# mLSTM branch: row sums from ones stored beside the values, and row maxima broadcast by DMA through DRAM

## The chip, the cores and the metric

The kernel runs on one core of a Trainium2 chip. A core has a matrix engine (PE, whose weight loads are shown apart as PEld), a vector engine (DVE), a scalar engine (ACT), GpSimd (POOL), and a queue that only issues DMAs (SP). Matmuls write into PSUM accumulators; DVE and ACT read these and write SBUF; POOL works on SBUF and issues DMAs of its own. The metric is the device time of one execution in microseconds, as the median of several runs. Lower is better.

## The reference, cut to what matters

Two layers, each over 256 tokens of width 2048. A layer projects the normed input into four branches (S5, mLSTM, differential attention, memory cross-attention), gates each, projects it back and merges the four. Everything is in 32-bit floats.

The change touches the mLSTM branch. It has 4 heads of width 256. For head h, with the summed log forget gates `acum`, the input gates `ic` and the running row maximum `m_row`, the reference computes

```
dmat = where(causal, acum_q - acum_k + ic_k, -inf)
s    = (q @ k^T) * exp(dmat - m_row)
num  = s @ v                    den = sum over k of s
h    = num / max(|den|, exp(-m_row))
```

It does so in two chunks of 128 tokens with a carried state. The kernel computes both chunks at once, as three 128 x 128 blocks of the lower triangle: (chunk 0, chunk 0), (chunk 1 rows, chunk 0 keys) and (chunk 1, chunk 1).

## The kernel before, in words

**The main stream.** All weights (944 pieces, called units here, of 128 x 1024 numbers) are loaded in order by SP (`do_load`, L292), split by ACT into a rounded high part `wh` (L303) and by DVE into the rest `wl` (`tt`, L206), and multiplied in three matmuls per product (`mm3`, L356 to L358: high by high, high by low, low by high). `tok_group` uses 12 matmuls of 512 columns per unit, `chan_group` 24 of 256 columns. While PE works on unit i, the split of unit i + 3 (`LA` = 3) is being issued. These high and low parts are of a type that PE takes in one pass.

**The branches run in between.** Each branch is a Python generator. After every unit, `used()` calls `bg_step()`, which advances each live generator by one `yield`: one step per unit. What a step emits goes to each engine's queue behind everything emitted earlier, and each engine works through its queue in that order. `ticks(n, period, stages)` starts head i at step `i * period` and runs stage `f` of a head at its offset. The S5 branch (`s5_gen`) runs along at the same time, with priority behind the mLSTM.

**The mLSTM.** `ml_rows` (L955) computes, some 70 units ahead, a tile `R` (`mlR`) of 128 partitions x 256 tokens: rows 0 to 3 hold the key terms, rows 32 to 35 the row maxima for the denominator, rows 64 to 67 the negated maxima of the four heads. `ml_gen` (L993) transposes `R` on PE, keeps two small pieces, and then per head:

- `s_mm` (offset 0): one matmul with a column of the identity, broadcast over 128 columns, against `R`. It copies row 64 + h of `R` to all 128 partitions of a PSUM tile `pm` (256 columns). Then four matmuls for the scores `k^T q`, into another PSUM tile.
- `s_arg` (offset 1, DVE): three instructions that read `pm` and write the exponents into `mlE`; `s_exp` (ACT) and `s_mul` (DVE) turn them into `s`.
- `o_mm` (offset 6): for each of the three blocks a matmul of `mlE` with the 256 value columns of this head, and one with two columns of ones (`ones2`, in the constants tile `cst`), whose first column is the denominator.
- `o_den` to `y_l` (offsets 7 to 17): normalisation and transposes; the small root of `o_rs` (L434 to L444, L1069) runs on POOL.

These matmuls take plain 32-bit operands. In the trace every such matmul stands as two records (8 heads in all, so `mlR` has 16 records). All helpers share lines: `mmf` is L361, the transpose `tr` L364, DVE's helpers L206 to L214, ACT's L203.

The heads start 16 steps apart. The values `v` lie in `mlv`, 2 x 1024 numbers per partition, written by ACT from PSUM when the value projection of a group of two heads is done.

**POOL's queue** carries the S5 branch's loads (`ur`, `br`, `ct`, `ub`) and stores (`ydr`) as DMAs, the small roots, and a few memsets. **PSUM** has three rotating buffers (`ps`) for all this work.

Of the kernel before, what the change touches and what calls it, by code (L numbers as in the profile page):

```python
# [8 lines left out]
F32 = mybir.dt.float32  # L9
# [148 lines left out]
def body(tc, x, mem, w_in, w_if, w_kv, w_br, w_glu, w_out, cols, s5_b, s5_c, lqk, g_post, consts, out,  # L158
         depth=L, taps=None):
    nc = tc.nc  # L160
    taps = taps or {}
    from contextlib import ExitStack
    with ExitStack() as ctx:
# [791 lines left out]
        def ml_rows(cl, wif, hb, lb, st):  # L955

            yield
            yield
            ifp = acc()
            for kb in range(16):  # L960
                nc.tensor.matmul(ifp[0:100, 0:256], lhsT=wif[:, kb, 0:100], rhs=hb(kb), start=kb == 0, stop=False,
                                 skip_group_check=True)
                nc.tensor.matmul(ifp[0:36, 0:256], lhsT=wif[:, kb, 0:36], rhs=lb(kb), start=False, stop=kb == 15,
                                 skip_group_check=True)
            yield
            bi, bf = pcol(cl, "b_i", 0, 4), pcol(cl, "b_f", 0, 4)
            w = [t2.tile([4, 2, 256], F32, name=f"mlw{i}", tag="t2") for i in range(2)]
            fr, ab, ee, A = w[0][:, 0], w[0][:, 1], w[1][:, 0], w[1][:, 1]
            S.copy(out=fr, in_=ifp[32:36, 0:256])
            S.copy(out=ab, in_=ifp[0:4, 0:256])  # L970
            R = sp.tile([128, 256], F32, name="mlR", tag="mlR")
            P.memset(R, 0.0)
            yield
            stt(fr, ifp[96:100, 0:256], bf, fr, A_, A_)
            stt(R[0:4], ifp[64:68, 0:256], bi, ab, A_, A_)
            ts(fr, fr, -1.0, M_)
            yield
            stt(ab, fr, -1.0, fr, M_, X_)
            act(ee, ab, AF.Exp, scale=-1.0)
            act(ee, ee, AF.Ln, bias=c_one[0:4])  # L980
            yield
            one = C("ones")[0:4, 0:1].to_broadcast([4, 256])
            stt(ee, fr, 0.0, ee, X_, A_)
            V.tensor_tensor_scan(out=A, data0=one, data1=ee, initial=0.0, op0=M_, op1=S_)
            tt(R[0:4], R[0:4], A, S_)
            yield
            V.tensor_tensor_scan(out=ab, data0=one, data1=R[0:4], initial=0.0, op0=M_, op1=X_)
            tt(R[32:36], A, ab, A_)
            ts(R[64:68], ab, -1.0, M_)
            st["R"] = R  # L990
            yield

        def ml_gen(l, cl, st, q8, k8, v, gate, yh, yl):  # L993
            R = st["R"]
            pc = ps()[:, 0:256]
            for t in range(2):
                tr(pc[:, t * 128:t * 128 + 128], R[:, t * 128:t * 128 + 128])
            pcv = pc.rearrange("p (t r) -> p t r", t=2)
            hg = sp.tile([128, 8], F32, name="mlhg", tag="mlhg")
            ts(hg, cl[:, COLS["ml_g"][0]:COLS["ml_g"][1]], 0.5, M_)  # L1000
            G = sp.tile([128, 2, 4], F32, name="mlG", tag="mlG")
            eam = sp.tile([128, 2, 4], F32, name="mleam", tag="mleam")
            V.tensor_copy(G, pcv[:, :, 0:4])
            act(eam, pcv[:, :, 32:36], AF.Exp, scale=-1.0)
            msk = C("maskml")
            yield
            held = {}

            def s_mm(h):
                pm = ps()[:, 0:256]  # L1010
                mmf(pm, ident[:, 64 + h:65 + h].to_broadcast([128, 128]), R, True, True)
                p = ps()[:, 0:384]
                for d in range(2):
                    mmf(p[:, 0:256], k8[:, 2 * h + d, 0:128], q8[:, 2 * h + d, 0:256], d == 0, d == 1)
                for d in range(2):
                    mmf(p[:, 256:384], k8[:, 2 * h + d, 128:256], q8[:, 2 * h + d, 128:256], False, d == 1)
                held[h] = {"pm": pm, "p": p}

            def s_arg(h):
                e = held[h]  # L1020
                pm = e["pm"]
                E = t2.tile([128, 384], F32, name="mlE", tag="t2")
                stt(E[:, 0:128], pm[:, 0:128], G[:, 0, h:h + 1], msk, A_, ALU.min)
                ts(E[:, 128:256], pm[:, 128:256], G[:, 0, h:h + 1], A_, 0.0, ALU.min)
                stt(E[:, 256:384], pm[:, 128:256], G[:, 1, h:h + 1], msk, A_, ALU.min)
                e["E"] = E

            def s_exp(h):
                act(held[h]["E"], held[h]["E"], AF.Exp)

            def s_mul(h):
                e = held[h]
                stt(e["E"], e["p"], 1.0 / 16, e["E"], M_, M_)

            def o_mm(h):
                E = held[h]["E"]
                vs = slice(h * 256, h * 256 + 256)
                pn = [ps(), ps()]
                mmf(pn[0][:, 0:256], E[:, 0:128], v[:, 0, vs], True, True)
                mmf(pn[0][:, 256:258], E[:, 0:128], ones2, False, True)  # L1040
                mmf(pn[1][:, 0:256], E[:, 128:256], v[:, 0, vs], True, False)
                mmf(pn[1][:, 256:258], E[:, 128:256], ones2, False, False)
                mmf(pn[1][:, 0:256], E[:, 256:384], v[:, 1, vs], False, True)
                mmf(pn[1][:, 256:258], E[:, 256:384], ones2, False, True)
                held[h]["pn"] = pn

            def o_den(h):
                e = held[h]
                rec = sm.tile([128, 2], F32, name="mlrec", tag="sm")
                dn = sm.tile([128, 2], F32, name="mldn", tag="sm")  # L1050
                for q in range(2):
                    V.tensor_copy(dn[:, q:q + 1], e["pn"][q][:, 256:257])
                stt(rec, dn, -1.0, dn, M_, X_)
                tt(rec, rec, eam[:, :, h], X_)
                V.reciprocal(out=rec, in_=rec)
                e["rec"] = rec

            def o_sq(h):
                e = held[h]
                y = t2.tile([128, 2, 256], F32, name="mly", tag="t2")  # L1060
                ss = sm.tile([128, 2], F32, name="mlss", tag="sm")
                for q in range(2):
                    act(y[:, q], e["pn"][q][:, 0:256], AF.Square, scale=e["rec"][:, q:q + 1], accum_out=ss[:, q:q + 1])
                e.update(y=y, ss=ss)

            def o_rs(h):
                e = held[h]
                rsqrt(e["ss"], e["ss"], 1.0 / 256, 2, P)
                P.tensor_tensor(out=e["ss"], in0=e["ss"], in1=e["rec"], op=M_)  # L1069

            def o_y(h):
                e = held[h]
                for q in range(2):
                    stt(e["y"][:, q], e["pn"][q][:, 0:256], e["ss"][:, q:q + 1], gate[:, q, h * 256:h * 256 + 256], M_, M_)

            def y_T(h):
                py = ps().rearrange("p (d t) -> p d t", d=2)
                for d in range(2):
                    for q in range(2):
                        tr(py[:, d, q * 128:q * 128 + 128], held[h]["y"][:, q, d * 128:d * 128 + 128])  # L1080
                held[h]["py"] = py

            def y_h(h):
                for d in range(2):
                    act(yh[:, 2 * h + d], held[h]["py"][:, d], AF.Identity, scale=hg[:, 2 * h + d:2 * h + d + 1])

            def y_l(h):
                for d in range(2):
                    stt(yl[:, 2 * h + d], held[h]["py"][:, d], hg[:, 2 * h + d:2 * h + d + 1], yh[:, 2 * h + d], M_, S_)

            yield from ticks(4, 16, [(0, s_mm), (1, s_arg), (2, s_exp), (4, s_mul), (6, o_mm), (7, o_den), (8, o_sq),
                                     (9, o_rs), (12, o_y), (15, y_T), (16, y_h), (17, y_l)])

        def xa_gen(l, qT, kT, v, z, yh, yl):
# [66 lines left out]
        ydr = dr.tile([8, 128, 256], F32, name="ydr")  # L1161
        kdr = dr.tile([128, 2048], F32, name="kdr")
        vdr = dr.tile([128, 2048], F32, name="vdr")

        def seq(*fns):

# [50 lines left out]
        for l in range(depth):  # L1217
# [93 lines left out]

            mlst = {}
            bg_add(ml_rows(cl, wif, hb, lb, mlst))
            mv = big("mlv").rearrange("p (t d) -> p t d", t=2)
            mg = big("mlg").rearrange("p (t d) -> p t d", t=2)

            def z_gen(o, g):
# [11 lines left out]
            for c0, dst, fn in ((MLV, mv, AF.Copy), (MLO, mg, AF.Tanh), (MLZ, None, None)):  # L1329
                for g in range(2):  # L1330
# [1 line left out]
                    if dst is None:  # L1332
                        bg_add(z_gen(o, g))
                    else:
                        evac(lambda o=o, g=g, dst=dst, fn=fn: [
                            act(dst[:, t, g * 512:g * 512 + 512], o[t], fn, scale=0.5 if fn == AF.Tanh else 1.0)
                            for t in range(2)])
            cq = big("mlq").rearrange("p (b t) -> p b t", b=8)
            ck = big("mlk").rearrange("p (b t) -> p b t", b=8)

# [279 lines left out]
```

## Time and profile before

| | |
|---|---|
| median of 3 runs | 2814.99 us (2811.59 to 2815.05) |
| the profiled execution | 2815.6 us, of which its span is 2813.8 us |
| PE busy | 2796.6 us, 99% |
| DVE busy | 1999.0 us, 71% |
| ACT busy | 1491.1 us, 53% |
| POOL busy | 274.4 us, 10% |
| granted PE clock | 0.998 |
| the mLSTM heads in layer 0, layer 1 | about 590 to 790 us, 1988 to 2190 us |

Busy time on PE counts a matmul from its start to its modelled end, and matmuls overlap; what one costs is read from the distance between starts, or from the chain of work that ended last, which gives each matmul only the time by which it moves the end. Each engine's busy share over the span hides stages: what a change is worth is read in the stretch where it acts. A time in this text is counted from the start of the span.

### The profile page before, as it was taken

The numbers are of one execution on the slowest core, as the hardware profiler recorded it, in microseconds if no ns is written. First come the engines' busy times: TensorE is split into PE (matmuls) and PEld (weight loads), VectorE is DVE, ScalarE is ACT, GpSimd is POOL, SyncE is SP. The second block draws the span as 40 slices with busy tenths as digits, with TensorE's granted clock in tenths as the row PEclk, the third lists the DMA queues.
The fourth block names the chain that finished last, engine by engine and source line by source line (L and its number), as shares of the span: only waits on it lengthen the run. The fifth ranks groups of instructions, "written<-read, shape, count | busy, mean of one in ns | idle before, by whom it ended". The sixth has DMA issues, their size and how long they took to land.

```text
span 2813.8 us, 41302 instructions
## 1 busy us (share of the span) xinstructions
PE 2796.6 (99%) x15604; PEld 2422.6 (86%) x15604; DVE 1999.0 (71%) x3068; ACT 1491.1 (53%) x2116; POOL 274.4 (10%) x594
## 2 busy tenths in 40 slices
PE   9999999999999999999999999999999999999998
PEld 7988878988998898887889888789889988988887
DVE  6678787787778875555575787877887778665555
ACT  6445665465555544444454556655655555444443
POOL 1010122011110000000010102220112000000000
PEclk9999999999999999999999999999999999999999
DMA  7666556555565556556566665565555655566555
GB/s 253 222 207 200 171 163 196 189 181 189 174 223 178 180 188 209 189 188 225 211 221 212 208 195 175 165 196 184 190 183 175 224 166 189 191 209 203 189 189 183
DMA packets 164840, 547.31 MB, mean 195 GB/s; under 512 B 32192, under 2 KB 32576, under 8 KB 162336
## 3 DMA queue, kind: packets, MB, share of 16 engines
q1 hardware_dynamic: 141408, 512.60, 54.5%
q0 software_dynamic: 23232, 32.08, 4.1%
q8 instruction: 122, 2.00, 0.3%
q14 instruction: 78, 0.64, 0.1%
HBM read 531.80 MB, written 12.58 MB: 193 GB/s over the span
## 4 chain that ended last, share of the span: by engine, by line
PE 96%; DVE 2%; issue 0%; DMA 0%; POOL 0%; ACT 0%; SPq 0%; DVEq 0%; ACTq 0%; POOLq 0%
PE acc L356 30%; PE acc L357 30%; PE acc L358 30%; PE ps L361 3%; PE ps L364 2%; DVE wl L206 1%; PE yps L361 1%; PE ps L753 1%; DMA memt<-in_mem 0%; ACT wh L303 0%; POOL rz L442 0%; DVE s5b L206 0%; DVE s5a L206 0%; DVE o L214 0%; DVE das L214 0%
## 5 line engine op out<-in xcount | busy, mean ns | idle before, releaser
L206 DVE TENSOR_TENSOR wl<-raw,wh 128x1024 fp32r<-128x1024 f32 x942 | 1150.7, 1223 | 755.8 <-ACT wh L303 752.1
L303 ACT CAST wh<-raw 128x1024 fp32r<-128x1024 f32 x942 | 987.9, 1050 | 1212.8 <-PE acc L358 814.3
L356 PE MATMUL acc<-wh,hh 128*128 128x512 f32 x1920 | 759.1, 395 | 0.0
L357 PE MATMUL acc<-wl,hh 128*128 128x512 f32 x1920 | 748.5, 390 | 0.5 <-DVE wl L206 0.5
L358 PE MATMUL acc<-wh,hl 128*128 128x512 f32 x1920 | 748.4, 390 | 0.0
L356 PE MATMUL acc<-hh,wh 128*128 128x256 f32 x1536 | 435.7, 284 | 0.0
L357 PE MATMUL acc<-hl,wh 128*128 128x256 f32 x1536 | 434.6, 283 | 0.0
L358 PE MATMUL acc<-hh,wl 128*128 128x256 f32 x1536 | 434.6, 283 | 0.0
L356 PEld LDWEIGHTS acc<-wh,hh 128*128 128x128 f32 x1920 | 360.8, 188 | 78.5 <-issue 6.5
L358 PEld LDWEIGHTS acc<-wh,hl 128*128 128x128 f32 x1920 | 360.4, 188 | 76.8
L357 PEld LDWEIGHTS acc<-wl,hh 128*128 128x128 f32 x1920 | 361.0, 188 | 71.2 <-DVE wl L206 1.1
L356 PEld LDWEIGHTS acc<-hh,wh 128*128 128x128 f32 x1536 | 294.8, 192 | 1.9 <-issue 1.6
L357 PEld LDWEIGHTS acc<-hl,wh 128*128 128x128 f32 x1536 | 294.8, 192 | 0.2
L358 PEld LDWEIGHTS acc<-hh,wl 128*128 128x128 f32 x1536 | 294.8, 192 | 0.0
L356 PE MATMUL acc<-wh,th 128*128 128x512 f32 x248 | 98.2, 396 | 0.0
L357 PE MATMUL acc<-wl,th 128*128 128x512 f32 x248 | 97.2, 392 | 0.0
L358 PE MATMUL acc<-wh,tl 128*128 128x512 f32 x248 | 97.1, 392 | 0.0
L674 POOL DMA_DIRECT2D ur<-udr x64 | 44.4, 693 | 515.0 <-DVE bs L206 491.2
L203 ACT ACT_TABLE_LOAD x67 | 86.0, 1283 | 6.7 <-DMA cols<-in_cols 3.3
L434 POOL TENSOR_SCALAR rq<-rq 128x2 f32<-128x2 f32 x28 | 7.3, 261 | 789.4 <-DVE rz L430 789.4
L771 DVE TENSOR_TENSOR_SCAN s5b<-s5r,s5a 128x256 f32<-128x256 f32 x128 | 81.1, 674 | 0.1
L356 PE MATMUL acc<-mh,wh 128*128 128x256 f32 x256 | 73.8, 288 | 0.0
(314 smaller groups left out, 3742.6 us busy)
## 6 DMA issues: line engine op xcount, KB each, us to landing
raw<-in_w_in SPq DMA_DIRECT2D x672, 512.0 KB, 3.4
raw<-in_w_br SPq DMA_DIRECT2D x128, 512.0 KB, 3.4
raw<-in_w_kv SPq DMA_DIRECT2D x64, 512.0 KB, 3.4
raw<-in_w_out SPq DMA_DIRECT2D x64, 512.0 KB, 3.3
raw<-in_w_glu SPq DMA_DIRECT2D x16, 512.0 KB, 4.3
ur<-udr POOLq DMA_DIRECT2D x64, 96.0 KB, 5.0
br<-in_s_b POOLq DMA_DIRECT2D x64, 96.0 KB, 5.6
memt<-in_mem SPq DMA_DIRECT2D x16, 256.0 KB, 7.0
```

The lines of the kernel that those rows point to most:

```text
L203: return S.activation(out=out, in_=in_, func=func, **kw)
L206: return V.tensor_tensor(out=out, in0=a, in1=b, op=op)
L303: S.copy(out=h, in_=r)
L356: nc.tensor.matmul(o, lhsT=ah, rhs=bh, start=start, stop=False, skip_group_check=True)
L357: nc.tensor.matmul(o, lhsT=ah, rhs=bl, start=False, stop=False, skip_group_check=True)
L358: nc.tensor.matmul(o, lhsT=al, rhs=bh, start=False, stop=stop, skip_group_check=True)
L361: nc.tensor.matmul(o, lhsT=lhsT, rhs=rhs, start=start, stop=stop, skip_group_check=True)
L364: nc.tensor.transpose(o, i, ident)
L434: E.tensor_scalar(out=m, in0=m, scalar1=-0.5, scalar2=None, op0=M_)
L674: nc.gpsimd.dma_start(out=ur, in_=udr[c // 4, rows].unsqueeze(0).to_broadcast([3, 32, 256]))
L753: nc.tensor.matmul(pb[:, ri], lhsT=e["bs"][:, ri], rhs=e["us"], start=ri == 0, stop=True, skip_group_check=True)
L771: V.tensor_tensor_scan(out=e["tb"][:, ri], data0=rb, data1=e["ta"][:, ri], initial=0.0, op0=M_, op1=A_)
```

## The change

Three things are done differently.

- **Ones beside the values.** `mlv` becomes 128 x 2 x 4 x 258: behind the 256 values of each head stand two columns of ones, written once per layer by a memset on POOL. ACT's writes into `mlv` become two blocks of 256 with a gap. `o_mm` then needs one matmul of 258 columns per block in place of one of 256 and one of 2, so its denominator arrives in column 256 of the same PSUM tile as before.
- **Row maxima by DMA.** At the end of `ml_rows` POOL's queue writes rows 64 to 67 of `R` to a DRAM buffer `rdr` (4 x 256). In `ml_gen` a new stage `r_load(h)` loads row h from there into all 128 partitions of an SBUF tile `mlpm` (128 x 256, one buffer). The matmul that made `pm` in PSUM is gone, and `s_arg` reads `mlpm`. Head 0 is loaded before the heads start, head h + 1 at offset 9 of head h.
- **Two steps later.** Behind the first `r_load` stand two extra `yield`s, so that all stages of all heads come two units later in the stream.

```diff
@@ ml_rows
             st["R"] = R
+            nc.gpsimd.dma_start(out=rdr, in_=R[64:68])
             yield
@@ ml_gen
+            def r_load(h):
+                pm = t1.tile([128, 256], F32, name="mlpm", tag="mlpm", bufs=1)
+                nc.gpsimd.dma_start(out=pm, in_=rdr[h].partition_broadcast(128))
+                held[h] = {"pm": pm}
+
             def s_mm(h):
-                pm = ps()[:, 0:256]
-                mmf(pm, ident[:, 64 + h:65 + h].to_broadcast([128, 128]), R, True, True)
                 p = ps()[:, 0:384]
                 ...
-                held[h] = {"pm": pm, "p": p}
+                held[h]["p"] = p
...
                 pn = [ps(), ps()]
-                mmf(pn[0][:, 0:256], E[:, 0:128], v[:, 0, vs], True, True)
-                mmf(pn[0][:, 256:258], E[:, 0:128], ones2, False, True)
-                mmf(pn[1][:, 0:256], E[:, 128:256], v[:, 0, vs], True, False)
-                mmf(pn[1][:, 256:258], E[:, 128:256], ones2, False, False)
-                mmf(pn[1][:, 0:256], E[:, 256:384], v[:, 1, vs], False, True)
-                mmf(pn[1][:, 256:258], E[:, 256:384], ones2, False, True)
+                mmf(pn[0][:, 0:258], E[:, 0:128], v[:, 0, h], True, True)
+                mmf(pn[1][:, 0:258], E[:, 128:256], v[:, 0, h], True, False)
+                mmf(pn[1][:, 0:258], E[:, 256:384], v[:, 1, h], False, True)
...
+            r_load(0)
+            for _ in range(2):
+                yield
             yield from ticks(4, 16, [(0, s_mm), (1, s_arg), ..., (8, o_sq),
+                                     (9, lambda h: h < 3 and r_load(h + 1)),
                                      (9, o_rs), (12, o_y), (15, y_T), (16, y_h), (17, y_l)])
@@ the layer's body
-            mv = big("mlv").rearrange("p (t d) -> p t d", t=2)
+            mv = b8.tile([128, 2, 4, 258], F32, name="mlv", tag="b8")
+            P.memset(mv[:, :, :, 256:258], 1.0)
...
+                                if dst is mv:
+                                    act(mv[:, t, 2 * g:2 * g + 2, 0:256], blk2(o[t]), AF.Copy)
```

On PE, the value product `o_mm` of head 0 in layer 0 stood in the queue like this before (each row is one matmul or a run of equal ones; `mlE` holds `s`, `cst` the ones):

```order
L358 MATMUL acc<-wh,hl 128x512
L361 MATMUL ps<-mlv,mlE 128x256
L361 MATMUL ps<-cst,mlE 128x2
L361 MATMUL ps<-mlv,mlE 128x256
L361 MATMUL ps<-cst,mlE 128x2
L361 MATMUL ps<-mlv,mlE 128x256
L361 MATMUL ps<-cst,mlE 128x2
L356 MATMUL acc<-wh,ydah 128x512
L357 MATMUL acc<-wl,ydah 128x512
```

and so with the change:

```order
L357 MATMUL acc<-wl,ydah 128x512
L358 MATMUL acc<-wh,ydal 128x512
L361 MATMUL ps<-mlv,mlE 128x258 x3
L356 MATMUL acc<-wh,ydah 128x512
L357 MATMUL acc<-wl,ydah 128x512
```

Six matmuls became three, and they stand two units further on. In `s_mm` of the same head (`mlR` is `R`, `mlq` and `mlk` the queries and keys) PE had before

```order
L358 MATMUL acc<-wh,hl 128x512
L361 MATMUL ps<-mlR,cst 128x256
L361 MATMUL ps<-mlq,mlk 128x256 x2
L361 MATMUL ps<-mlq,mlk 128x128 x2
L356 MATMUL acc<-wh,hh 128x512
```

and has with the change

```order
L358 MATMUL acc<-wh,hl 128x512
L361 MATMUL ps<-mlq,mlk 128x256 x2
L361 MATMUL ps<-mlq,mlk 128x128 x2
L356 MATMUL acc<-wh,hh 128x512
```

so only the matmul that reads `R` is gone. POOL's queue, around the loads for heads 0 and 1 in layer 0, reads with the change as follows (in brackets the engines and DMA queues whose progress a row waits for):

```order
L802 DMA ydr<-ub 128x256 [waits DMASW7_49,DVE_49]
L1012 DMA mlpm<-rdr 128x256 [waits DMASW0_49]
L674 DMA ur<-udr 96x1x256 [waits DMASW3_49,DVE_49,Activation_49]
L675 DMA br<-in_s_b 96x1x256 [waits DMASW4_49,DVE_49,Activation_49]
L666 DMA ct<-in_s_c 128x256 [waits PE_49]
L667 DMA ub<-udr 128x256 [waits DMASW7_49]
L674 DMA ur<-udr 96x1x256 [waits DMASW5_49,DVE_49,Activation_49]
L675 DMA br<-in_s_b 96x1x256 [waits DMASW6_49,DVE_49,Activation_49]
L1012 DMA mlpm<-rdr 128x256 [waits DMASW0_49,DVE_49]
L434 TENSOR_SCALAR rq<-rq 128x2 [waits DVE_49]
```

The two rows of L1012 are new; the second stands ahead of the small root of head 0 and waits for DVE, since `mlpm` has one buffer that `s_arg` of head 0 must have read.

More of the change, by code (lines that the diff above doesn't have):

```diff
@@ L1036, in o_mm @@
                 E = held[h]["E"]
-                vs = slice(h * 256, h * 256 + 256)
                 pn = [ps(), ps()]
-                mmf(pn[0][:, 0:256], E[:, 0:128], v[:, 0, vs], True, True)
-                mmf(pn[0][:, 256:258], E[:, 0:128], ones2, False, True)
-                mmf(pn[1][:, 0:256], E[:, 128:256], v[:, 0, vs], True, False)
-                mmf(pn[1][:, 256:258], E[:, 128:256], ones2, False, False)
-                mmf(pn[1][:, 0:256], E[:, 256:384], v[:, 1, vs], False, True)
-                mmf(pn[1][:, 256:258], E[:, 256:384], ones2, False, True)
+                mmf(pn[0][:, 0:258], E[:, 0:128], v[:, 0, h], True, True)
+                mmf(pn[1][:, 0:258], E[:, 128:256], v[:, 0, h], True, False)
+                mmf(pn[1][:, 0:258], E[:, 256:384], v[:, 1, h], False, True)
                 held[h]["pn"] = pn
@@ L1163, in body @@
         vdr = dr.tile([128, 2048], F32, name="vdr")
+        rdr = dr.tile([4, 256], F32, name="rdr")
         def seq(*fns):
@@ L1334, in body, with ev @@
                     else:
-                        evac(lambda o=o, g=g, dst=dst, fn=fn: [
-                            act(dst[:, t, g * 512:g * 512 + 512], o[t], fn, scale=0.5 if fn == AF.Tanh else 1.0)
-                            for t in range(2)])
+                        def ev(o=o, g=g, dst=dst, fn=fn):
+                            for t in range(2):
+                                if dst is mv:
+                                    act(mv[:, t, 2 * g:2 * g + 2, 0:256], blk2(o[t]), AF.Copy)
+                                else:
+                                    act(dst[:, t, g * 512:g * 512 + 512], o[t], fn, scale=0.5)
+                        evac(ev)
             cq = big("mlq").rearrange("p (b t) -> p b t", b=8)
```

## The prediction

> **What bounds the kernel now.** I read the page first, then PE's own waits, then the two stretches of the first mLSTM (590 to 690 and 690 to 790 us) by engine, and last the chain of waits inside them.
>
> ```profile
> span 2813.8 us, 41302 instructions
> PE 2796.6 (99%) x15604; PEld 2422.6 (86%) x15604; DVE 1999.0 (71%) x3068; ACT 1491.1 (53%) x2116; POOL 274.4 (10%) x594
> PE 96%; DVE 2%; issue 0%; DMA 0%; POOL 0%; ACT 0%; SPq 0%; DVEq 0%; ACTq 0%; POOLq 0%
> ```
>
> PE is the bound: it fills the span, and the chain that ended last runs over it for 96%. All that PE waited for in the whole program is this:
>
> ```profile
> PE ps L364 <- DMA memt<-in_mem: 3.4, 2, 2.1
> PE ps L364 <- DVE ydal L214: 2.0, 2, 1.0
> PE ps L361 <- DVE warm L1201: 1.3, 1, 1.3
> PE acc L357 <- DVE wl L206: 0.8, 3, 0.3
> ```
>
> Columns are total us, times, longest. None of these is in the mLSTM heads. There, by stretch (us, then busy us of PE, PEld, DVE, ACT, POOL, clock, DMA share, GB/s):
>
> ```profile
> 590.00:690.00 100.00, 100.00 (x472) 82.73 (x471) 84.23 (x148) 60.49 (x86) 17.53 (x39) 1.00 0.58 184
> 690.00:790.00 100.00, 100.00 (x669) 91.78 (x668) 77.87 (x132) 54.33 (x79) 16.57 (x39) 1.00 0.56 182
> ```
>
> PE has no gap, and the clock is full. So whatever work leaves PE here shortens the program, as long as DVE, which is 84% busy, still delivers the splits `wl` in time. And nothing but shorter PE work can help here: there is no idle time to recover.
>
> **What the removed matmuls cost.** Their records:
>
> ```profile
> L361 PE MATMUL ps<-mlv,mlE 128*128 128x256 f32 x48 | 15.2, 406 | 0.0
> L361 PE MATMUL ps<-cst,mlE 128*128 128x2 f32 x48 | 6.7, 209 | 0.0
> L361 PE MATMUL ps<-mlR,cst 128*128 128x256 f32 x16 | 4.7, 378 | 0.0
> ```
>
> The counts give 24 value products, 24 products with ones and 8 products with `R`, two records each. Adding the busy times of the last two (6.7 + 4.7 = 11.4 us) would overstate the price, since records overlap. The chain gives each group only the time by which it moves the end (start, us, what, records). For `s_mm` and `o_mm` of head 0, each with the matmuls right behind it:
>
> ```profile
> 593.49 1.74 PE ps L361 x10
> 595.23 0.24 PE acc L356
> 595.46 0.23 PE acc L357
> 611.85 1.86 PE ps L361 x12
> 613.71 0.34 PE acc L356
> 614.04 0.23 PE acc L357
> ```
>
> And as a yardstick, `s_mm` of the memory attention, which is four plain 32-bit matmuls of 256 columns and nothing else:
>
> ```profile
> 835.30 1.73 PE ps L361 x8
> 837.03 0.23 PE acc L356
> ```
>
> One such matmul costs 1.73 / 4 = 0.4325 us, and the matmul behind the group pays nothing extra (0.23).
>
> - `R` matmul: 0.43 us per head. `s_mm` goes from 1.74 to 1.31. The four score matmuls stay.
> - Ones: `o_mm` now takes 1.86, of which three value products are 3 x 0.4325 = 1.30; the three pairs of two-column records make up the other 0.56, 0.19 us a pair for 2 columns. Behind them the first matmul of the main stream takes 0.34 in place of 0.23, 0.11 more; behind a group that ends in a wide matmul (837.03, 595.23) it doesn't. So 0.56 + 0.11 = 0.67 per head.
> - The two columns that each value product gains: 2 / 256 of 0.4325 is 0.003 us, 0.01 per head. No row shows a plain matmul of 258 columns. From below it costs the 0.4325 of 256 columns, from above the 0.43 + 0.19 + 0.04 = 0.66 that the pair costs today (if the extra columns were worked off as a piece of their own). I take 0.436, since cost per column is even between the rows at hand, and keep the other end for a rival.
>
> Sum per head: 0.43 + 0.67 - 0.01 = 1.09 us. Eight heads: **8.7 us** off PE.
>
> [...]
>
> **What is added, and what hides it.** DVE's three instructions of `s_arg` now read SBUF.
>
> ```profile
> L214 DVE SCALAR_TENSOR_TENSOR mlE<-ps,mlG,cst 128x128 f32<-128x128 f32 x16 | 5.5, 341 | 0.0
> L206 DVE TENSOR_TENSOR us<-ur,us x64: 416/417/419, 175.0 to 2432.9; 32x256 fp32r<-32x256 f32 x64
> L206 DVE TENSOR_TENSOR lq<-lq x4: 217/218/225, 272.0 to 1672.0; 128x64 f32<-128x64 f32 x4
> ```
>
> From PSUM one takes 0.34; from SBUF, 64 columns take 0.22 and 256 take 0.42, so 128 lie between: at most 8 x 3 x 0.08 = 1.9 us more on DVE over the program, at most 2.9 less. I take nothing. ACT writes the same 512 numbers per instruction into `mlv`, only with a gap in them; I take nothing there too.
>
> Whether DVE's work is hidden is a matter of the lead with which a split is ready. Counting splits and units from the start (944 of each), the smallest lead in either layer's heads is this one:
>
> ```profile
> 728.83 1.23 DVE L206 TENSOR_TENSOR wl<-raw,wh 128x1024 fp32r<-128x1024 f32 x1 [2.11 <-ACT wh L303]
> 733.66 0.28 PE L357 MATMUL acc<-hl,wh 128*128 128x256 f32 x1
> ```
>
> Ready at 730.06, used at 733.66: 3.6 us. Most others have 5 to 8. PE takes 1.1 us per head less, once in 16 units, and DVE catches up within a head, as it is idle for 16 of 100 us. So the lead covers the faster PE, and the two-step shift of every stage merely moves the same DVE work among other splits.
>
> POOL gets 8 loads, 2 stores and 2 small memsets. The nearest transfers are the S5 loads, and `lq`, which copies one row of 256 numbers to 128 partitions just as the new load does (KB, us from issue to landing; then the least, median and most for `ur`):
>
> ```profile
> ur<-udr POOLq DMA_DIRECT2D x64, 96.0 KB, 5.0
> lq<-in_lqk POOLq DMA_DIRECT2D x2, 128.0 KB, 4.9
> DMA to landing us min/median/max: 3.4/5.0/7.1
> 575.87 0.57 POOL L667 DMA_DIRECT2D ub<-udr  x1
> 622.03 0.22 POOL L434 TENSOR_SCALAR rq<-rq 128x2 f32<-128x2 f32 x1 [45.59 <-DVE rz L430]
> ```
>
> `mlpm` lands some 5 us (3.4 to 7.1) after its issue. For head 0 POOL stood idle from 576 to 622 us, and its load waits only for a store made 200 us earlier; `s_arg` runs after 598. For the others the load is emitted 8 steps ahead of `s_arg`; a step is 12 matmuls of 0.23 us, so 8 are 22 us. Cover is 22 - 0.6 - 5 = 16 us, and if that were used up, the 3.6 us of lead would come next. Behind the load in POOL's queue stands only the root of the head before, needed three steps (8 us) later. So the price is nothing.
>
> The store of `R` and the memset fall into the one stretch where PE is short of splits:
>
> ```profile
> 381.12 0.50 PE L357 MATMUL acc<-wl,hh 128*128 128x512 f32 x1 [0.27 <-DVE wl L206]
> 378.63 0.28 DVE L210 TENSOR_SCALAR mlR<-mlw 4x256 f32<-4x256 f32 x1
> 385.23 0.23 POOL L434 TENSOR_SCALAR rq<-rq 128x2 f32<-128x2 f32 x1 [20.30 <-DVE rz L430]
> ```
>
> The store can go at 379 and takes under 0.8 us of POOL, which sits idle until 385. If it came 0.6 us in the way in both layers, it would cost 1.2 us; I take nothing and keep that.
>
> **Sum.** The profiled execution took 2815.6 us, 1.8 around its span. 2815.6 - 8.7 = 2806.9. It stands 0.6 above the median of the runs, so the median of the changed kernel should be **2806.3 us**, 0.31% less. A difference of 0.2% (5.6 us) is about what a measurement of this kernel can tell from no change.
>
> **The rivals.**
>
> - *The splits run out.* In 590 to 690 us, where heads 0 and 1 run, DVE is 84% busy. If the faster PE ate the lead there, PE would wait for `wl` and the first two heads of each layer would give their gain back: 4 x 1.09 = 4.4 us, time 2810.7. For it: the DVE share, and PE has waited for `wl` at 381 us. Against: leads of 3.6 us and more against 1.1 per head. Chance 0.10.
> - *A 258-column matmul costs as much as the pair.* Then only the `R` matmul pays, 8 x 0.43 = 3.5 us: 2811.5. This is also the case in which the ones were never worth removing. Nothing in the rows shows a step in cost at 256 columns. Chance 0.05.
> - *Two-column records are nearly free*, by their columns, and the 0.56 us belongs to something that stays, such as the change between operand types. Then 3.5 us from `R` and the 0.11 behind each `o_mm`, 0.9: 2810.6. Against: the yardstick group changes types as well and leaves nothing over. [...] Chance 0.05.
> - *The broadcast comes late, and the kernel is slower.* `s_arg` would hold DVE's queue, the split of the next unit stands behind it, and PE starves. It begins when `mlpm` lands more than 22 us after its turn, and costs PE from 22 + 3.6 on; the kernel is slower by over 0.2% when each head loses 1.09 + 0.7, that is at 27.4 us and more. At 30 us: 8 x (4.4 - 1.09) = 26 us, 2841. For it: every load is issued by POOL, in a queue that also waits for DVE (`ub`, `ur`), while DVE is 84% busy. [...] Chance 0.06.
>
> That the change doesn't do what it says can be left out: PE's list has 32 matmuls less.
>
> **How the numbers follow.** The forecast has what is left, 0.74: full gain, 2806.3, and within it 2803 to 2809 by the spread of the runs before (2811.6 to 2815.1) and the 1.2 us kept above. The range takes in the three small-gain cases: 2802.0 to 2811.6. Faster by over 0.2%: the forecast's 0.74 less 0.03 for its upper edge, plus 0.02 of the first rival, 0.73. Within 0.2%: 0.21. Slower: 0.06.
>
> **What would show it.** The chain should show `s_mm` at 1.31 us with 8 records, `o_mm` at 1.30 to 1.31 with 6, and 0.23 to 0.24 for the matmul behind it. PE's waits should hold no row for `wl` in the heads, and DVE none for `mlpm`. `mlpm` should land in about 5 us. DVE's and ACT's busy time should stay within 3 us. An `o_mm` of 1.9 us, or a row in which DVE waits for `mlpm`, would make the prediction wrong.

## The result, and the profile after

The changed kernel takes 2830.68 us (median of 4 runs, 2830.36 to 2833.67) against 2814.27 of the kernel before (4 runs, 2811.59 to 2815.05). The ratio is 1.0064, with a 95% interval of 1.0048 to 1.008: **slower by 0.6%**, where 0.31% less was forecast.

Read part by part, the forecast steps are all there. The head of the page of the changed kernel, and all that PE waited for:

```profile
span 2831.9 us, 41192 instructions
PE 2814.6 (99%) x15540; PEld 2406.0 (85%) x15540; DVE 1999.3 (71%) x3068; ACT 1493.8 (53%) x2116; POOL 281.5 (10%) x606
...
PE 96%; DVE 2%; issue 0%; DMA 0%; POOL 0%; ACT 0%; SPq 0%; DVEq 0%; ACTq 0%; POOLq 0%
```

```profile
PE ps L364 <- DMA memt<-in_mem: 3.8, 3, 2.0
PE ps L364 <- DVE ydal L214: 2.0, 2, 1.0
PE ps L361 <- DVE warm L1206: 1.3, 1, 1.3
PE acc L357 <- DVE wl L206: 0.7, 2, 0.5
```

PE has 64 records less, waits about as long as before (7.8 us in place of 7.5), and is busy 18 us longer. The chain of waits gives `s_mm` and `o_mm` of head 0 as follows (start, us, what, records):

```profile
602.57 1.31 PE ps L361 x8
603.88 0.24 PE acc L356
...
620.90 1.30 PE ps L361 x6
622.20 0.24 PE acc L356
```

1.31 and 1.30, as forecast. So the heads gained what they should, and some other place lost about three times as much. It shows in the costliest groups of the page (busy us, then mean ns of one). These rows are of the kernel before,

```profile
L356 PE MATMUL acc<-wh,hh 128*128 128x512 f32 x1920 | 759.1, 395 | 0.0
L357 PE MATMUL acc<-wl,hh 128*128 128x512 f32 x1920 | 748.5, 390 | 0.5 <-DVE wl L206 0.5
L358 PE MATMUL acc<-wh,hl 128*128 128x512 f32 x1920 | 748.4, 390 | 0.0
L356 PE MATMUL acc<-hh,wh 128*128 128x256 f32 x1536 | 435.7, 284 | 0.0
```

and these of the changed one:

```profile
L356 PE MATMUL acc<-wh,hh 128*128 128x512 f32 x1920 | 768.3, 400 | 0.0
L358 PE MATMUL acc<-wh,hl 128*128 128x512 f32 x1920 | 757.9, 395 | 0.0
L357 PE MATMUL acc<-wl,hh 128*128 128x512 f32 x1920 | 756.1, 394 | 0.0
...
L356 PE MATMUL acc<-hh,wh 128*128 128x256 f32 x1536 | 430.5, 280 | 0.0
```

The main stream, which the change doesn't touch, has another pace: by these means a matmul of 512 columns lasts 4 to 5 ns longer, one of 256 columns 4 ns less. That holds far from the heads too. By stretch, main-stream matmuls alone (us, busy us and their number; 100 to 140 us holds only matmuls of 256 columns, 180 to 260 us only such of 512; behind them clock, DMA share, GB/s), before

```profile
100.00:140.00 40.00, 40.00 (x336) 1.00 0.72 249
180.00:260.00 80.00, 77.25 (x335) 1.00 0.60 191
```

and changed:

```profile
100.00:140.00 40.00, 40.00 (x341) 1.00 0.72 252
180.00:260.00 80.00, 77.25 (x328) 1.00 0.57 185
```

The clock (1.00) and PE's share are equal; 335 against 328 is 2.1% less work done in the same time. Adding the distances between the starts of neighbouring main-stream matmuls over the whole trace (8259 pairs of 512 columns, 5715 of 256) gives 1897.0 + 688.0 us before and 1934.7 + 678.0 after: +37.7 and -10.0, so +27.7. Less the 9 us gained in the heads that is +18.6, and the spans differ by 18.1. The whole miss lies there.

**What moved.** The 14 buffers of the pool `b8` are as large as the largest tile that any of them holds. `mlv` grew from 8192 bytes per partition to 8256, so all 14 did. `hh`, `hl`, `mh`, `th`, `gh` and the other activations of the main stream live in that pool. Before, buffer k began at byte 67168 + 8192 k, and `wh` and `wl` at bytes 34400 + 4096 i and 50784 + 4096 i: all of them 96 more than a multiple of 256. With the change, buffer k begins 64 k bytes later; the buffers that `hh` uses are displaced against the weights by 64 and 64 bytes modulo 256 in layer 0, by 0 and 192 in layer 1. By the addresses in the two builds, 10,516 of the 14,208 main-stream matmuls have an activation that is displaced against its weights, none did before.

### The profile page after: what moved, and what is told of

Its sections match the earlier page's. It is cut to its first block, busy times and chain, and to the rows that moved or that the text cites. A ratio compares the mean times of both kernels' runs of the same rounds, so it can differ in the third digit from the quotient of the medians.

```text
span 2831.9 us, 41192 instructions
## 1 busy us (share of the span) xinstructions
PE 2814.6 (99%) x15540; PEld 2406.0 (85%) x15540; DVE 1999.3 (71%) x3068; ACT 1493.8 (53%) x2116; POOL 281.5 (10%) x606
## 4 chain that ended last, share of the span: by engine, by line
PE 96%; DVE 2%; issue 0%; DMA 0%; POOL 0%; ACT 0%; SPq 0%; DVEq 0%; ACTq 0%; POOLq 0%
PE acc L357 30%; PE acc L356 30%; PE acc L358 30%; PE ps L361 3%; PE ps L364 1%; DVE wl L206 1%; PE yps L361 1%; PE ps L753 1%; DMA memt<-in_mem 0%; ACT wh L303 0%; POOL rz L442 0%; DVE s5b L206 0%; DVE s5a L206 0%; DVE o L214 0%; DVE das L214 0%
## 5 line engine op out<-in xcount | busy, mean ns | idle before, releaser
L356 PE MATMUL acc<-wh,hh 128*128 128x512 f32 x1920 | 768.3, 400 | 0.0
L358 PE MATMUL acc<-wh,hl 128*128 128x512 f32 x1920 | 757.9, 395 | 0.0
L357 PE MATMUL acc<-wl,hh 128*128 128x512 f32 x1920 | 756.1, 394 | 0.0
L357 PEld LDWEIGHTS acc<-hl,wh 128*128 128x128 f32 x1536 | 288.8, 188 | 0.3
L358 PEld LDWEIGHTS acc<-hh,wl 128*128 128x128 f32 x1536 | 288.6, 188 | 0.0
L357 PE MATMUL acc<-ml,wh 128*128 128x256 f32 x256 | 71.9, 281 | 0.0
```

Source lines behind the costliest of these rows:

```text
L356: nc.tensor.matmul(o, lhsT=ah, rhs=bh, start=start, stop=False, skip_group_check=True)
L357: nc.tensor.matmul(o, lhsT=ah, rhs=bl, start=False, stop=False, skip_group_check=True)
L358: nc.tensor.matmul(o, lhsT=al, rhs=bh, start=False, stop=stop, skip_group_check=True)
```

## The experiments

My theory was then: the 64 bytes set the pace. The rivals: the DMA broadcast, the extra columns or the shift by two steps slow the stream in a way not seen in waits.

**1 to 3: the bytes alone, and the change without them.** `pad64` is the kernel before with a longer tile:

```diff
-            mv = big("mlv").rearrange("p (t d) -> p t d", t=2)
+            mv = b8.tile([128, 2064], F32, name="mlv", tag="b8")[:, 0:2048].rearrange("p (t d) -> p t d", t=2)
```

> The kernel before, with one difference: the tile mlv is allocated 64 bytes per partition longer, and the extra bytes are never touched. As all 14 buffers of its pool have the size of the largest tile, each starts 64 bytes later than the one before it, as in the changed kernel; no instruction is added, removed or moved. Layout theory (the buffers' addresses slow the main stream's matmuls): 512-column matmuls of the main stream go from 229.7 to about 234.3 ns apart, those of 256 columns from 120.4 to 118.6, so 8259 x 4.6 - 5715 x 1.8 = +28 us: about 2842 us. Rival (the broadcast by DMA, the ones or the two-step shift slow PE in some way): no difference, 2814 us.

`dma_only` has the DMA broadcast and the two steps, and keeps `mlv` and the matmuls with ones:

```diff
+            nc.gpsimd.dma_start(out=rdr, in_=R[64:68])
...
-                mmf(pm, ident[:, 64 + h:65 + h].to_broadcast([128, 128]), R, True, True)
...
+            r_load(0)
+            for _ in range(2):
+                yield
```

> The change without the ones: row maxima by DMA and the two-step shift, while mlv and o_mm are as before, so the pool's buffers stay 8192 bytes. Layout theory: the main stream keeps its pace and the removed R matmuls pay 8 x 0.43 = 3.5 us: 2811 us. Rival that the loads or the shift are what slows PE: 2825 us or more.

`both_8192` is the whole change with the buffers at 8192 bytes: seven of the eight blocks of 258 columns fit, and the eighth gets a small tile of its own.

```diff
-            mv = b8.tile([128, 2, 4, 258], F32, name="mlv", tag="b8")
+            mvt = big("mlv")
+            mv7 = t1.tile([128, 258], F32, name="mlv7", tag="mlv7", bufs=1)
+            mvs = mvt[:, 0:1806].rearrange("p (i c) -> p i c", c=258)
+            def mv(t, h):
+                return mv7 if (t, h) == (1, 3) else mvs[:, 4 * t + h]
```

> The whole change, but the pool's buffers keep 8192 bytes: seven of the eight value blocks of 258 columns lie in the old tile, the eighth (second chunk, head 3) in a small tile of its own. Layout theory: pace of the main stream as before, and the 8.7 us of the sum come out: 2805.5 us. Rival (the change itself costs time on PE): about 2830 us.

Measured, against 2813.03 us of the kernel before (the ratio of the changed kernel is the one above, against 2814.27):

| | us | ratio (95%) | 512 columns, 256 columns: mean distance, ns |
|---|---|---|---|
| before | 2813.03 | | 229.68, 120.39 |
| changed kernel | 2830.68 | 1.0064 (1.0048 to 1.008) | 234.25, 118.64 |
| `pad64` | 2840.06 | 1.0097 (1.008 to 1.0113) | 234.03, 118.61 |
| `dma_only` | 2809.76 | 0.9989 (0.998 to 0.9998) | 229.66, 120.39 |
| `both_8192` | 2803.95 | 0.9969 (0.9958 to 0.998) | 229.56, 120.43 |

The stretches of `pad64`, whose instructions are those of the kernel before, one for one:

```profile
100.00:140.00 40.00, 40.00 (x342) 1.00 0.72 251
180.00:260.00 80.00, 77.25 (x329) 1.00 0.58 184
```

and those of `both_8192`, which has the whole change:

```profile
100.00:140.00 40.00, 40.00 (x336) 1.00 0.72 249
180.00:260.00 80.00, 77.25 (x335) 1.00 0.60 189
```

So 64 unused bytes cost 27 us, and without them the change gains 9.1 us. The changed kernel itself is 9.4 us faster than `pad64`, whose buffers lie as its own do: the gain is there, on top of the loss. The pace goes with the bytes, not with the DMA, the ones or the steps.

**4: is it the place of the operands?** `pace1` leaves the whole computation out; it runs only matmuls in the order of the main stream, in 58 settings, with `wh`, `wl`, `hh` and `hl` displaced by chosen bytes within one region. It ran once.

```diff
+def tok(wh, wl, hh, hl, units, cols=128, n=512):
+    ...
+    mm(o, at(hh + so, cols), at(wh + mo, n), f, False)
+    mm(o, at(hh + so, cols), at(wl + mo, n), False, False)
+    mm(o, at(hl + so, cols), at(wh + mo, n), False, g)
```

> Leaves the whole computation out: only matmuls of the main stream's two kinds on one SBUF tile, 48 of 512 columns or 96 of 256 per case, with the addresses of the two operands' tiles moved against each other by 0 to 4096 bytes per case; the output is the last accumulators. Layout theory: 227 and 120 ns apart at displacement 0 and some other numbers, from about 226 to 240 and from 113 to 127, at displacements that are multiples of 64. If the pace were a matter of other engines' traffic, which is absent here, all cases would take the same time.

Mean distances, ns, by the displacement of both activations against the weights (the first twelve distances of each case left out):

| bytes | 0 | 4 | 8 | 16 | 32 | 64 | 96 | 128 | 192 | 256, 512, 1024, 2048, 4096 |
|---|---|---|---|---|---|---|---|---|---|---|
| 512 columns | 226.7 | 232.4 | 230.7 | 233.3 | 233.4 | 233.4 | 234.3 | 232.4 | 229.0 | 226.7 |
| 256 columns | 120.0 | 123.3 | 120.0 | 118.7 | 116.6 | 117.8 | 119.9 | 120.0 | 117.8 | 120.0 |

With all four moved by 64 bytes together it is 226.7 and 120.0 again; with `wl` alone moved by 64 it is 232.1 and 117.8, with `hl` alone 231.0 and 117.8. After the first 43 us no other engine works in this program until its end, so the pace is a matter of PE's own two operands: of their relative place, with a period of 256 bytes as far as tried (256 to 4096 bytes give the pace of 0). At displacement 0 every single distance of 512 columns is 226 or 227 ns; elsewhere they vary from one matmul to the next (231 to 236 at 64 bytes).

**5 to 7: the same in the kernel itself.** Unused bytes are put ahead of a pool of the kernel before. In `shift64` they move the activations by 64 bytes, in `shift256` by 256; in `all64` they stand further ahead, so that weights and activations move by 64 together. The edit of `shift64`

```diff
         wlp = pool("wlp", LA + 1)
+        padp = pool("padp", 1)
+        pad = padp.tile([128, 16], F32, name="pad", tag="pad")
         b8 = pool("b8", 14)
```

(with 64 numbers in place of 16 in `shift256`), and in `all64`

```diff
         sp = pool("sp", 1)
+        padp = pool("padp", 1)
+        pad = padp.tile([128, 16], F32, name="pad", tag="pad")
         rawp = pool("rawp", 4)
```

> The kernel before with 64 unused bytes per partition ahead of the pool of 14 buffers, so that all of them start 64 bytes later against the weight tiles wh and wl, and their distance from each other stays 8192 bytes (one memset of the 64 bytes is added). By the paces measured alone (displacement 64: 233.4 ns for 512 columns and 117.8 for 256, at 0: 226.7 and 120.0) 8259 x 6.7 - 5715 x 2.2 = +43 us: 2856 us. Rival, that the irregular distance of 8256 between the buffers is what counts and not their place against the weights: no difference, 2813 us.

> The kernel before with 256 unused bytes ahead of the pool of activations (where 64 unused bytes gave 2848.6 us). If only the place of the activations against the weights modulo 256 bytes counts, this is the kernel before again: 2813 us, mean distances of the matmuls 229.7 ns (512 columns) and 120.4 ns (256 columns). If it were the unused tile, or any move of the pool, that costs, it would come near 2848.

> The kernel before with 64 unused bytes ahead of the incoming weights, so that weights, their high and low parts and the activations all move by 64 bytes together. If the relative place counts, 2813 us. If the place in the memory itself counts, as 64 bytes did for the activations alone, near 2848.

| | us | before, us | ratio (95%) | 512, 256 columns, ns |
|---|---|---|---|---|
| `shift64` | 2848.6 | 2812.44 | 1.0126 (1.0096 to 1.0155) | 235.27, 118.16 |
| `shift256` | 2813.47 | 2813.61 | 0.9999 (0.9989 to 1.0008) | 229.40, 120.39 |
| `all64` | 2813.09 | 2813.61 | 0.9998 (0.9988 to 1.0007) | 229.43, 120.38 |

The stretches of `shift64`,

```profile
100.00:140.00 40.00, 40.00 (x342) 1.00 0.73 252
180.00:260.00 80.00, 77.26 (x327) 1.00 0.58 184
```

and of `shift256`:

```profile
100.00:140.00 40.00, 40.00 (x336) 1.00 0.74 248
180.00:260.00 80.00, 77.25 (x335) 1.00 0.60 189
```

The same unused tile costs 36 us at 64 bytes and nothing at 256, and 64 bytes cost nothing where the weights move along. That settles what sets the pace: the relative place of weights and activations modulo 256 bytes. Why it does so stays open (last section). The size was expected too large by 7 us: `pace1` gives 512 columns 6.7 ns more, the kernel shows 5.6.

**8 to 11: can the place be used?** `pace2`, again with the computation left out and again a single run, goes through all 512 combinations of displacements in steps of 32 bytes.

> Leaves the whole computation out, as in the run of paces before: 512 settings of the low part wl of the weights and of the high and low part of the activations, each displaced by 0 to 224 bytes in steps of 32 against the high part of the weights, 24 matmuls of 512 columns and 48 of 256 for each. Expected by the paces so far: the 512-column kind is fastest (226.7) where all displacements are 0 and 229 to 235 elsewhere; the 256-column kind is slowest or near it there (120.0) and reaches 116 to 117 elsewhere. If a setting other than 0 gives the 512-column kind less than 226, the layout of the kernel before is not its best.

For 512 columns nothing was less than 226.7 ns, which only two combinations reached: no displacement, and `wl` by 160 with `hl` by 128 bytes. All others took 228.8 to 236.7. For 256 columns it went from 113.3 to 124.5 ns, with 120.0 at no displacement, where some nine tenths of the 512 combinations are faster. So the kernel before lies at the best place for its long matmuls and near the slowest for its short ones, and the two can be parted, since each unit of weights is used by one kind only: in `chan224` the buffers of `wh` and `wl` are 4352 bytes, and units for matmuls of 256 columns begin at byte 224 of them.

```diff
-                h = whp.tile(shape3(i), F32R, name="wh", tag="wh")
-                lo = wlp.tile(shape3(i), F32R, name="wl", tag="wl")
+                o = 56 if chan[i] else 0
+                h = whp.tile([128, 1088], F32R, name="wh", tag="wh")[:, o:o + 1024].rearrange("p (k n) -> p k n", k=2)
+                lo = wlp.tile([128, 1088], F32R, name="wl", tag="wl")[:, o:o + 1024].rearrange("p (k n) -> p k n", k=2)
```

> The kernel before (neither part of the change), with weight tiles wh and wl of 4352 bytes, of which the units that go to 256-column matmuls use the 4096 bytes from byte 224 on and all others the first 4096. The 512-column kind stays at displacement 0, the 256-column kind gets the activations 32 bytes (modulo 256) ahead of the weights. Layout theory, by the paces measured alone (116.6 for 120.0 ns in both runs of them): 5715 x 3.4 = 19.4 us less, 2793 us. If the pace in the kernel follows something else than these places, 2813 us.

`both_s192` is `both_8192` with 192 unused bytes ahead of the activations:

```diff
+        padp = pool("padp", 1)
+        pad = padp.tile([128, 48], F32, name="pad", tag="pad")
         b8 = pool("b8", 14)
```

> The whole change with buffers of 8192 bytes, and 192 unused bytes ahead of the pool, so that all activations are displaced by 192 bytes against the weights. The two runs of paces differ here: 229.0 and 117.8 ns in the first (+6.4 us over displacement 0, so 2810 us), 228.9 and 113.3 in the second (-19.5 us, so 2784 us). The run tells which of the two paces the 256-column kind takes in the kernel.

`chan64_dma` joins the DMA broadcast of `dma_only` with the parted weights, here at byte 64:

```diff
+                o = 16 if chan[i] else 0
...
-                pm = t1.tile([128, 256], F32, name="mlpm", tag="mlpm", bufs=1)
+                pm = sp.tile([128, 256], F32, name="mlpm", tag="mlR")
```

> A version meant to be faster than both: the row maxima by DMA (without the ones, for which no room is left), mlpm in the place of R, which is free by then, and weight tiles of 4352 bytes as in the run chan224, but units for 256-column matmuls use the 4096 bytes from byte 64 on, so that activations stand 192 bytes (modulo 256) ahead of the weights. In both_s192 this setting gave 115.6 ns for the 256-column kind, against 120.4; the 512-column kind stays at displacement 0. Layout theory: 5715 x 4.8 = 27.4 us and 3.4 us of the R matmuls off 2813: 2782 us. If the 256-column kind falls into the 117.8 ns that the same setting took in the first run of paces, 2794 us.

| | us | before, us | ratio (95%) | 512, 256 columns, ns |
|---|---|---|---|---|
| `chan224` | 2794.42 | 2813.05 | 0.9933 (0.9916 to 0.995) | 229.53, 117.17 |
| `both_s192` | 2791.59 | 2813.05 | 0.9922 (0.9907 to 0.9937) | 231.47, 115.60 |
| `chan64_dma` | **2783.94** | 2814.08 | 0.989 (0.9874 to 0.9907) | 229.50, 115.67 |

The stretches of `chan64_dma`:

```profile
100.00:140.00 40.00, 40.00 (x356) 1.00 0.77 261
180.00:260.00 80.00, 76.32 (x329) 1.00 0.57 186
```

In its 40 us of short matmuls 356 stand in place of 336. (The second row holds fewer, because after the faster short stage 16 records of the S5 branch (`yps`) come into it, which in the kernel before start only at 263 us: PE's time on the main stream there is 76.32 us in place of 77.25.) `chan224` and `chan64_dma` met their forecasts within 2 us; `both_s192` fell between its two, since both of its paces are there. `pace1` has 117.8 ns for 256 columns at 192 bytes and `pace2` 113.3; of the 5705 distances in `both_s192` 3436 are 113 or 114 ns and 2204 are 117 to 119. A pace holds for many matmuls on end: in `chan64_dma` 100 to 140 us, with 40.00 us busy, has 356 of them (some 113 ns each), and 495 to 530 us, with 34.93 us busy, has 300 (some 117). So the displacement alone doesn't fix the pace here; what decides between the two isn't shown. `chan64_dma` took over the mean of 115.6 from `both_s192`, and its mix came out alike (3305 and 2345): that this forecast held to 2 us was luck in part. `chan64_dma` beats both kernels, by 1.1% against before. The ones beside the values aren't in it: buffers of 4352 bytes and the 258-column blocks don't fit together beside the kernel's other tiles.

## Why the prediction was wrong, step by step

- *PE bounds, and whatever leaves it shortens the program.* Right: PE's waits in the changed kernel sum to about the same few us, and in `both_8192` the time falls by what was taken off.
- *`R` matmul, 0.43 us per head, 3.5 us in all.* Right: `dma_only` gains 3.3 us (interval 0.6 to 5.6), and `s_mm` takes 1.31.
- *Ones, 0.67 per head less 0.01 for the wider matmuls, 5.3 us.* Right: from `dma_only` to `both_8192` it is 5.8 us, and 1.30 for three matmuls of 258 columns is 0.433 each, the price of 256. For head 0 `dma_only`, which keeps the ones, has (start, us, what, records)

```profile
616.27 1.86 PE ps L361 x12
618.12 0.34 PE acc L356
```

  and `both_8192`

```profile
615.98 1.30 PE ps L361 x6
617.28 0.23 PE acc L356
```

  The rival in which 258 columns cost as much as the pair falls, and so does the one of nearly free short records: with its 3.5 + 0.9 = 4.4 us `both_8192` would have gained less than the 5.6 us at which its interval begins.
- *The sum of 8.7 us.* As a price for the matmuls it holds: 9.1 us in `both_8192`.
- *DVE and ACT at nothing, the loads hidden.* Right, by these rows of the changed kernel's `mlE` and `mlpm` (ns, least, median and most; then us):

```profile
L214 DVE SCALAR_TENSOR_TENSOR mlE<-mlpm,mlG,cst x16: 342/346/352, 608.5 to 2157.3; 128x128 f32<-128x128 f32 x16
DMA to landing us min/median/max: 3.2/3.5/4.9
```

  346 ns from SBUF against 341 from PSUM (the third instruction of `s_arg` takes 281 against 342); DVE 1999.3 us busy (1999.0 before), ACT 1493.8 (1491.1); no wait of DVE for `mlpm` anywhere, and a landing of 3.5 us where about 5 was taken. The rival of a late broadcast, the only one on the slower side, played no part.
- *The splits keep up.* Right: neither in the changed kernel nor in `both_8192` does PE wait for a split while the heads run. What `both_8192` has in all,

```profile
PE acc L357 <- DVE wl L206: 1.9, 5, 0.8
PE acc L356 <- ACT wh L303: 0.6, 1, 0.6
```

  lies outside them, 2.0 of the 2.5 us in the first 100 us of the program. `shift256`, which has no part of the change, waits 1.7 us there. The rival that gave back 4.4 us in the heads didn't come.

- *The step that failed* is the inventory of the change. Of `mlv` the prediction priced what ACT writes into it ("the same 512 numbers per instruction", at nothing) and what PE reads of it, but not its size. 64 bytes more in a tile of a rotating pool displace 10 of its 14 buffers against the weights (all but numbers 0, 4, 8 and 12), and with them activations of 10,516 matmuls. That term, +27.7 us by the distances and +27.0 by `pad64`, was missing, and none of the rivals held it, since all of them looked for a cost at the mLSTM.
- *"Nothing but shorter PE work can help here: there is no idle time to recover."* Wrong. A PE without a gap and at full clock still had 30 us to give (`chan64_dma`), of which only 3 are work removed. A busy share of 100% says that the next matmul is always there, not that it is taken at its best pace: 40.00 busy us of 40.00 hold 336 short matmuls before and 356 in `chan64_dma`.

No row of before could have warned of it, since there all operands of the main stream had one relative place throughout. The size of the tile stood in the diff, and what it moves in the addresses that the two builds give; both were there ahead of the run and weren't weighed.

## What to carry to other kernels

Where a change alters the size of any tile of a shared pool, or adds a pool, compare the addresses of the matmul operands before and after, modulo 256 bytes (here a move by 64 cost 36 us in `shift64`, one by 256 nothing in `shift256`), and price a move by the number of matmuls that it touches. When a local change makes work elsewhere faster or slower, compare the mean duration and the count per stretch of untouched instructions first. To test a layout effect, pad the kernel before and change nothing else; and try the paddings on purpose, since the place that a kernel happens to have need not be its best (2794.42 us in `chan224` against 2813.05).

## What was not expected of the hardware

In `pace1`, with both operands at the same place modulo 256 bytes, one matmul follows the other in 120.0 ns (256 columns), 173.3 (384) and 226.7 (512): 0.417 ns a column and 13.3 ns besides. At other places the 13.3 ns change, to 20 for 512 columns (233.4 at 64 bytes) and, in `pace2`, down to 6.6 for 256 (113.3). They do so in patterns that repeat over several matmuls (226, 229, 232 ns at 192 bytes), and the 256-column kind has two lasting paces at that place (113 or 114 ns and 117 to 119 in `both_s192`). Halving the loaded columns to 64 at displacement 0 didn't shorten the distance but gave 230.1 ns.

What in PE or in the memory makes the place count is open; no run shows it. What `pace2` shows is that the pace depends on where the one operand lies against the other, by up to 4% for 512 columns (226.7 to 236.7 ns) and 10% for 256 (113.3 to 124.5).
